# Down projection of a conformer/SSD block: 16 of its 22 k tiles as seven block products in two passes, in place of eight

## The chip, the cores and the metric

The kernel runs on one core of a Trainium2 chip. The metric is the device time of one execution in microseconds (us). It was run three times: 1059.66, 1051.93 and 1051.59 us, with a median of 1051.93. One further execution was profiled, and all rows below come from it.

The engines are named as the profile names them: PE is the matrix engine (PEld its weight loads), DVE the vector engine, ACT the scalar engine, POOL the GpSimd engine, SP the engine that issues the weight loads. PSUM has eight banks of 128 x 512 fp32; SBUF is the working memory.

## The reference, cut to what matters

The whole is one block of a hybrid network: a gated convolution branch, a state-space branch, a mixing projection, and a feed-forward part. Only the last lines bear on the change:

```
h = rms_norm(x, ffn_pre_g[i])                       # x: 512 tokens x 1024
gt, up = jnp.split(h @ w_gate_up[i], 2, axis=-1)    # FFN_HIDDEN = 2816
f = (jax.nn.silu(gt) * up) @ w_down[i]              # 512 x 2816 @ 2816 x 1024
x = x + rms_norm(f, ffn_post_g[i])
```

The down projection is the last product. Its contraction has 2816 = 22 x 128 rows, the 22 k tiles.

## The kernel before, in words

**Three matmuls for one.** Each fp32 operand is split into a high part (a rounding copy on ACT) and a low part (the rest, a subtraction on DVE). `mm3` (L171) multiplies high x high, high x low and low x high into the same PSUM bank; these are the matmuls of L173, L174 and L175. So each 128 x 512 piece of weights costs one ACT copy and one DVE subtraction per tile of 128 x 1024 (L139 and L145, or L905 and L910 where the gate/up projection does it), and each k tile of the activation costs one of each at 128 x 512 (L1200, L1201). For some weight tiles the low part is formed differently: ACT writes the negated high part, and a DMA from POOL's queue adds the weights on top while it copies (L142 and L143, or L907 and L908).

**Order.** `ORDER` is the list of all weight tiles in the order of their loads. `w_raw` (L129) issues a load on SP's queue into one of five `raw` buffers (`RAW_BUFS`); a load waits until the tile five places before it has been read for the last time. The split tiles lie in two sets of buffers, five pairs `whi`/`wlo` and three pairs `chi`/`clo`, which `pair_of_tiles` (L889) hands out in turn. The program is written in a sequential order, and the framework places every instruction in its engine's queue: it takes what its own timing says is ready, and the written order decides between what is ready together. Within a queue an engine works in order. `not_before` (L166) ties the order of two instructions by hand.

**Gate/up projection.** Its 22 units u (L1181 to L1194) are already done as seven block products in place of eight: `prep_s` (L924) and `prep_a` (L918) form sums of weight blocks on DVE and their halves, and `product` (L953) accumulates one block product. The activations' sums are in 14 tiles of the pool `h2`. The result of silu(gate) x up is `f32`, 22 k tiles of 128 x 512 tokens.

**Down projection.** After unit 21 the pool `h2` is closed (L1209), and in its place come `xres` (the residual, loaded by ACT's queue at L1212), `gpost1`, and four buffers each for the halves of `f32`. The first two k tiles' halves (`f01`, L1195) and the first two weight tiles (L1205) are formed before the last products of the gate/up projection. All eight PSUM banks hold the output: four token tiles t times two halves n of the 1024 columns. For k = 0 to 18 all eight banks take a step (`f_step`, L1220: 24 matmuls of 128 x 512); for the last three k the loop runs over t and n, so that each bank is finished in turn. Each finished token tile is squared on ACT (`mean_sq`, L838), its scale is made on DVE and POOL (`factor`, L844: L848 and L849), multiplied by the gain (L1249), added to the residual (L1237) and stored (L1240).

Of the kernel before, what the change touches and what calls it, by code (L numbers as in the profile page):

```python
# [18 lines left out]
P = 128  # L19
T = 512  # L20
# [57 lines left out]
ADD_LO = (2, 3) + tuple(range(7, FF // P, 2))  # L78
GU_AHEAD = 5
MOV_AT = 192  # L80

TAPS_GLU = 12
TAPS = (6, 14, 18, 20, 20, 20, 20, 20)
# [16 lines left out]
ORDER += [("wd", _i) for _i in range(NF)]  # L100


ZZ_LAST = [("zz", 4 * _p + 3) for _p in range(G // 2 - 1)]
# [8 lines left out]
def block_kernel(ctx: ExitStack, tc: tile.TileContext, x, xT, x0, prm, hp, gp, w, out):  # L112
# [11 lines left out]

    raws, split, more_raw = {}, {}, []
    seq = {key: n for n, key in enumerate(ORDER)}
    GU = range(seq["gu", 0], seq["wd", 0])

    def w_raw(n):  # L129
        if n < len(ORDER) and n not in raws:  # L130
# [1051 lines left out]
    for u in range(NF):  # L1182
# [9 lines left out]
            x3(u)  # L1192
        prep_s(max(u + 1, 3))
        prep_a(max(u + 2, 4) if u else 3)  # L1194
    f01 = [t.rearrange("p (k t) -> p k t", k=2) for t in pair_of_tiles()]  # L1195
    fs = {}

    def f_halves(k, room):
        fs[k] = room
        act.copy(fs[k][0], f32[:, k, :])  # L1200
        dve.tensor_tensor(out=fs[k][1], in0=f32[:, k, :], in1=fs[k][0].bitcast(F32), op=ALU.subtract)  # L1201

    for k in range(2):
        f_halves(k, [f[:, k] for f in f01])
    wd_ahead = [w_split(seq[("wd", k)]) for k in range(2)]  # L1205
    v2(NF - 1)
    x4(NF - 1)
    mark["chain"] = False
    h2.close()  # L1209
    pf = ctx.enter_context(tc.tile_pool(name="pf", bufs=2))  # L1210
    xres = pf.tile([P, NT, D], F32, bufs=1, name="xres")
    nc.scalar.dma_start(xres, x2d.rearrange("(t p) d -> p t d", p=P))  # L1212
    gpost1 = pf.tile([P, D], F32, bufs=1, name="gpost1")
    nc.scalar.dma_start(gpost1, gp[1].partition_broadcast(P))

    def f_split(k):
        if k < NF and k not in fs:
            f_halves(k, [pf.tile([P, T], F32R, tag=f"f{p}", bufs=4, name=f"f{p}{k}") for p in "hl"])

    def f_step(ps, t, k, wt, ns=(0, 1)):  # L1220
        tok = slice((t % 2 * 2 + t // 2) * P, (t % 2 * 2 + t // 2 + 1) * P)
        tm_step(ps, t, k, NF, fs[k][0][:, tok], fs[k][1][:, tok], wt, ns)

    ps = tm_tiles("wd")
    last = 3
    for k in range(NF - last):
        wt = w_get("wd", k)
        for j in range(3):
            f_split(k + j)
        for t in range(NT):  # L1230
            f_step(ps, t, k, wt)
    ws = {k: w_get("wd", k) for k in range(NF - last, NF)}
    f_split(NF - 1)

    def store(t, mg, rs):
# [6 lines left out]
    for t in range(NT):  # L1242
        mg = pf.tile([P, D], F32, tag="mg", name=f"mgc{t}")
        for n, c in enumerate(cols2):
            for k in range(NF - last, NF):
                f_step(ps, t, k, ws[k], (n,))
        rs = scale_of(ps[t], pf, f"c{t}")
        for n, c in enumerate(cols2):
            dve.tensor_tensor(out=mg[:, c], in0=ps[t][n], in1=gpost1[:, c], op=ALU.mult)  # L1249
        if t:  # L1250
            store(t - 1, *done)
        done = (mg, rs)
    store(NT - 1, *done)


def _feature_major(wt, cols):
# [4 lines left out]
def _layout(inp):  # L1261
    x = inp["x"][0]
    w_in, pw, so = inp["w_in"][0], inp["conv_pw_w"][0], inp["ssm_out_w"][0]
    wo, wgu, wd = inp["w_out"][0], inp["w_gate_up"][0], inp["w_down"][0]
    zs = [_feature_major(w_in, slice(OFF_Z + g * GW, OFF_Z + (g + 1) * GW)) for g in range(G)]
    zd = np.concatenate([zs[0].reshape(P, NK, GW), _feature_major(w_in, slice(OFF_DT, OFF_GATE)).reshape(P, NK, H)], axis=2)
    strips = {
        "val": (w_in, 0), "glu": (w_in, D), "x": (w_in, OFF_XBC), "B": (w_in, OFF_B),
        "C": (w_in, OFF_C), "gc": (w_in, OFF_GATE), "gs": (w_in, OFF_GATE + D), "pw": (pw, 0),
    }  # L1270
    rows = {"wo": wo, "wd": wd}

    def piece(n, i):
        if n == "gu":
            u, j = i // 2, i % 2
            o = (u % 2) * FF + (u // 2) * 2 * P
            one, two = [_feature_major(wgu, slice(o + q * P, o + (q + 1) * P)) for q in range(2)]
            return one if j == 0 else two
        if n in strips:
            a, o = strips[n]  # L1280
            return _feature_major(a, slice(o + i * P, o + (i + 1) * P))
        if n == "zd":
            a = zd[:, 3 * i : 3 * i + 3].reshape(P, -1)
            return np.pad(a, ((0, 0), (0, D - a.shape[1])))
        if n == "z":
            return zs[1][:, i * D : (i + 1) * D]
        if n == "zz":
            a = [zs[2 * (i // 4) + 2 + j].reshape(P, NK, GW)[:, 2 * (i % 4) : 2 * (i % 4) + 2] for j in range(2)]
            return np.concatenate(a, axis=2).reshape(P, -1)
        if n == "so":  # L1290
# [43 lines left out]
```

## Time and profile before

| what | value |
|---|---|
| times of three runs | 1059.66, 1051.93, 1051.59 us |
| span of the profiled execution, first to last instruction | 1050.4 us |
| granted PE clock over the span | 0.999 |
| PE busy | 1040.4 us (99%) |
| PEld busy | 908.2 us (86%) |
| DVE busy | 764.4 us (73%) |
| ACT busy | 602.8 us (57%) |
| POOL busy | 89.3 us (9%) |
| DMA moved | 141.35 MB, mean 135 GB/s |
| first and last matmul of the down projection start | 923.97 and 1043.44 us |

The profile gives no time for the profiled execution besides its span; the two shorter runs are 1.2 and 1.5 us above that span, which is what lies around the first and last instruction.

How to read it: an instruction's duration runs from its start to its results being written, and the next instruction of the same engine starts a little before that. So what an engine can do in a stretch is counted by the distance from start to start, and what a dependent instruction waits for by the whole duration. In a row of a timeline, the first number is the start in us, the second the length in us, and a bracket at the end gives the idle time of the engine before it and what ended it. In a table of windows, each engine's busy us and, in brackets, its instructions stand behind the length of the window.

### The profile page before, as it was taken

What the parts mean: (1) busy time and instruction counts of PE and PEld (TensorE: products, weight loads), DVE (VectorE), ACT (ScalarE), POOL (GpSimd) and SP (SyncE); (2) the same over time, 40 slices, a digit from 0 to 9 for tenths busy, and PEclk for the clock granted to TensorE, in tenths of its full rate; (3) what the DMA queues carried; (4) which work ended last, traced back from release to release, by engine and by line L of the source; (5) the groups of instructions that cost most, each with busy time, mean ns of one, the idle gap of its engine ahead of it and who ended that gap; (6) DMA issues with size and microseconds to landing.
All of it is one profiled execution on the core that took longest, in us unless ns stands there. A gap on an engine that the chain in (4) does not pass through costs nothing.

```text
span 1050.4 us, 15167 instructions
## 1 busy us (share of the span) xinstructions
PE 1040.4 (99%) x5893; PEld 908.2 (86%) x5893; DVE 764.4 (73%) x1114; ACT 602.8 (57%) x1011; POOL 89.3 (9%) x114
## 2 busy tenths in 40 slices
PE   9999999999999999999999999999999999999997
PEld 7898889888888888888888888889999999988886
DVE  7899976968595969596976555479997987643334
ACT  7655978684867476834432582376675665533322
POOL 0101101110111011101000000010000000000000
PEclk9999999999999999999999999999999999999999
DMA  8567644656445545554353223434565453352202
GB/s 295 152 168 213 149 102 120 180 138 163 122 139 149 134 141 139 140 141 120 87 134 101 80 79 103 161 114 127 170 189 144 126 163 114 101 209 94 98 1 80
DMA packets 39816, 141.35 MB, mean 135 GB/s; under 512 B 4544, under 2 KB 5568, under 8 KB 38720
## 3 DMA queue, kind: packets, MB, share of 16 engines
q1 hardware_dynamic: 28656, 97.32, 27.6%
q0 software_dynamic: 8352, 34.61, 16.8%
q10 hardware_dynamic: 2736, 8.46, 2.2%
q8 instruction: 46, 0.75, 0.3%
q14 instruction: 26, 0.21, 0.1%
HBM read 136.10 MB, written 4.26 MB: 134 GB/s over the span
## 4 chain that ended last, share of the span: by engine, by line
PE 94%; DVE 3%; ACT 1%; DMA 0%; issue 0%; SPq 0%; POOL 0%; DVEq 0%; POOLq 0%; ACTq 0%
PE tm_wd L175 4%; PE tm_wd L174 4%; PE tm_wd L173 4%; PE xy L173 3%; PE xy L174 3%; PE xy L175 3%; PE pso L173 3%; PE px L175 3%; PE px L173 3%; PE pso L175 3%; PE pso L174 3%; PE px L174 3%; PE yd L613 3%; PE pz L174 2%; PE pz L175 2%; PE pz L173 2%
## 5 line engine op out<-in xcount | busy, mean ns | idle before, releaser
L139 ACT CAST whi<-raw 128x1024 fp32r<-128x1024 f32 (+2 forms) x138 | 138.0, 1011 | 187.7 <-PE pC L174 39.8
L423 DVE SCALAR_TENSOR_TENSOR a<-v,prm_t,a 128x511 f32<-128x511 f32 (+15 forms) x240 | 180.7, 755 | 10.6 <-ACT a L420 7.9
L145 DVE TENSOR_TENSOR wlo<-raw,whi 128x1024 fp32r<-128x1024 f32 (+2 forms) x98 | 112.9, 1156 | 56.7 <-ACT whi L139 55.2
L143 POOL DMA_DIRECT2D wlo<-in_w x40 | 35.7, 892 | 363.5 <-ACT jk L649 91.8
L173 PE MATMUL tm_wd<-whi,fh 128*128 128x512 f32 x160 | 62.2, 389 | 0.0
L174 PE MATMUL tm_wd<-wlo,fh 128*128 128x512 f32 x160 | 62.2, 389 | 0.0
L175 PE MATMUL tm_wd<-whi,fl 128*128 128x512 f32 x160 | 62.2, 389 | 0.0
L174 PE MATMUL pz<-wlo,hhi 128*128 128x512 f32 (+2 forms) x160 | 56.1, 353 | 0.1
L175 PE MATMUL pz<-whi,hlo 128*128 128x512 f32 (+2 forms) x160 | 56.0, 352 | 0.0
L173 PE MATMUL pz<-whi,hhi 128*128 128x512 f32 (+2 forms) x160 | 55.6, 354 | 0.0
L1201 DVE TENSOR_TENSOR fl<-f,fh 128x512 fp32r<-128x512 f32 x20 | 13.8, 691 | 50.3 <-ACT fh L1200 50.3
L173 PE MATMUL px<-hhi,whi 128*128 128x512 f32 x128 | 50.2, 392 | 0.0
L175 PE MATMUL px<-hhi,wlo 128*128 128x512 f32 x128 | 49.9, 390 | 0.0
L174 PE MATMUL pso<-yl,whi 128*128 128x512 f32 x128 | 49.8, 389 | 0.0
L174 PE MATMUL px<-hlo,whi 128*128 128x512 f32 x128 | 49.8, 389 | 0.0
L175 PE MATMUL pso<-yh,wlo 128*128 128x512 f32 x128 | 49.7, 389 | 0.0
L173 PE MATMUL pso<-yh,whi 128*128 128x512 f32 x128 | 49.6, 391 | 0.0
L905 ACT CAST whi_g<-raw 128x1024 fp32r<-128x1024 f32 x40 | 41.3, 1054 | 14.4 <-DVE raw L936 7.3
L1200 ACT CAST fh<-f 128x512 fp32r<-128x512 f32 x20 | 12.4, 620 | 60.4 <-PE tm_wd L174 60.4
L910 DVE TENSOR_TENSOR wlo_g<-raw,whi_g 128x1024 fp32r<-128x1024 f32 x34 | 41.2, 1223 | 5.1 <-ACT whi_g L905 5.0
L142 ACT ACTIVATE wlo<-whi 128x1024 fp32r<-128x1024 f32 x40 | 42.2, 1055 | 0.3
L406 ACT ACTIVATE L<-L,nacs 128x128 f32<-128x128 f32 x128 | 40.1, 391 | 3.4 <-POOL L L400 3.2
(458 smaller groups left out, 3207.8 us busy)
## 6 DMA issues: line engine op xcount, KB each, us to landing
raw<-in_w SPq DMA_DIRECT2D x176, 512.0 KB, 3.8
wlo<-in_w POOLq DMA_DIRECT2D x40, 512.0 KB, 5.8
L<-scr POOLq DMA_DIRECT2D x8, 1024.0 KB, 6.2
wlo_g<-in_w POOLq DMA_DIRECT2D x6, 512.0 KB, 6.5
xr<-in_x ACTq DMA_DIRECT2D x4, 512.0 KB, 5.6
x2d<-xr ACTq DMA_DIRECT2D x4, 512.0 KB, 2.6
clo_g<-in_w POOLq DMA_DIRECT2D x4, 512.0 KB, 5.9
xres<-x2d ACTq DMA_DIRECT2D x1, 2048.0 KB, 10.0
```

The lines of the kernel that those rows point to most:

```text
L139: act.copy(hi[:, c], src[:, c])
L142: act.activation(lo[:, c], hi[:, c].bitcast(F32), AF.Copy, scale=-1.0)
L143: mark["lo"] = pool.dma_start(lo[:, c], w[n][:, c].bitcast(F32R), accum_op=ALU.add)
L145: mark["wlo"] = dve.tensor_tensor(out=lo[:, c], in0=src[:, c], in1=hi[:, c].bitcast(F32), op=ALU.subtract)
L173: mark["pe"] = pe.matmul(ps, lh, rh, start=start, stop=False, skip_group_check=more)
L174: pe.matmul(ps, lh, rl, start=False, stop=False, skip_group_check=more)
L175: mark["pe3"] = pe.matmul(ps, ll, rh, start=False, stop=stop, skip_group_check=more)
L406: act.activation(L[:, h, c, :], L[:, h, c, :], AF.Exp, bias=nacs[:, c, HG * g + h : HG * g + h + 1])
L423: return dve.scalar_tensor_tensor(out=va[j][:, d:], in0=vs[j][:, : T - d], scalar=col("dw_w", j * KC + KC - 1 - d), in1=va[j][:, d:], op0= ...
L613: pe.matmul(yd[c // 2][:, c % 2, h, :], s["L"][:, h, c, :], s["xdt"][:, c, h, :], start=True, stop=True)
L905: a_ = act.copy(hi, src)
L910: d_ = dve.tensor_tensor(out=lo, in0=src, in1=hi.bitcast(F32), op=ALU.subtract)
```

## The change

Sixteen of the 22 k tiles are taken as four groups j of four tiles. In each group the tiles of even number are one half of the contraction, those of odd number the other; the 512 tokens and the 1024 columns are halved too. Of the eight products of halves seven remain, each of a sum of activation blocks with a sum of weight blocks (`quad`: 12 matmuls of 128 x 512, two k tiles, two token tiles, one column half). Each product is accumulated over all four j in its own pair of PSUM banks.

- Pass 1 has three products: `plain_1`, `third_1`, `second_1`, in banks A, C and B. Pass 2 has four: `first_2` in two new banks D, `plain_2` on top of A, `fourth_2` on top of C, `sum_2` in B again. Between the passes A is copied to SBUF by ACT, and B and C are folded into two SBUF tiles by DVE (`between`), which also frees B.
- The weights of the 16 tiles come as 24 loads in place of 16 (`w1`, `w2`: three blocks per j and pass); the other six k tiles are loaded as before.
- The sums are formed on DVE, partly in place in `f32` and in the `raw` tiles; one sum per j is kept in SBUF between the passes (`keep`).
- Every product needs halves of its weights (128 x 1024) and of its activations (128 x 512): `w_form`, `f_form`. In 11 of the 28 products (`plain_1` of j = 0, 2, 3, all `plain_2` and `fourth_2`) the low half of the weights is made by ACT and an adding DMA from POOL's queue.
- The products are listed in `steps`, and the forms of a step are written four steps ahead of its matmuls (`S_AHEAD`); `not_before` keeps the matmuls in the written order.
- Then the six remaining k tiles are added in the old manner, with the token tiles in the order 1, 3, 0, 2 and the column halves in the order 1, 0. For six of the eight banks a DVE instruction adds or subtracts an SBUF tile, and the squares are then taken from SBUF.
- The pool for `xres` and `gpost1` is opened after pass 2.

```diff
+NS2 = 4
+KS2 = 4 * NS2
+ORDER += [("w1", 3 * _j + _q) for _j in range(NS2) for _q in range(3)]
+ORDER += [("w2", 3 * _j + _q) for _j in range(NS2) for _q in range(3)]
+ORDER += [("wd", _i) for _i in range(KS2, NF)]
...
+    one, two = [f32[:, e : KS2 : 2, :] for e in range(2)]
+    def f_form(j, name, src, room=None):
+        hi, lo = F_[j, name] = room or f_room(f"{name}{j}")
+        act.copy(hi, src)
+        dve.tensor_tensor(out=lo, in0=src, in1=hi.bitcast(F32), op=ALU.subtract)
+    def w_form(j, name, src, again=None):
+        hi, lo = pair_of_tiles()
+        Wd[j, name] = hi, lo
+        act.copy(hi, src)
+        if again is not None:
+            act.activation(lo, hi.bitcast(F32), AF.Copy, scale=-1.0)
+            pool.dma_start(lo, w[again].bitcast(F32R), accum_op=ALU.add)
+        else:
+            dve.tensor_tensor(out=lo, in0=src, in1=hi.bitcast(F32), op=ALU.subtract)
...
+    def plain_1(j, room=None):
+        n, ra = w_next("w1", j, 0)
+        w_form(j, "a11", ra, n if j != 1 else None)
+        f_form(j, "b11", f_of(j, one, c1), room)
+    def third_1(j, tmp=None, room=None):
+        ...
+        dve.tensor_tensor(out=t3, in0=f_of(j, one, c2), in1=f_of(j, two, c2), op=ALU.subtract)
+        dve.tensor_tensor(out=rb_, in0=ra, in1=rb_, op=ALU.add)
+        f_form(j, "t3", t3, room)
+        w_form(j, "s3", rb_)
+    def second_1(j, room=None, kept=None):
+        dve.tensor_tensor(out=b12, in0=b12, in1=b11, op=ALU.subtract)
+        dve.tensor_tensor(out=b11, in0=b12, in1=f_of(j, two, c2), op=ALU.subtract)
+        dve.tensor_tensor(out=keep[j], in0=rb_, in1=rc, op=ALU.add)
+        f_form(j, "t2", b11, room)
+        w_form(j, "s2", keep[j])
+    def first_2(j):
+        dve.tensor_tensor(out=rb_, in0=rb_, in1=rc, op=ALU.add)
+        f_form(j, "t1", f_of(j, one, c2))
+        w_form(j, "s1", rb_)
+    def plain_2(j):
+        w_form(j, "a12", rd, n)
+        f_form(j, "b21", f_of(j, two, c1))
+    def fourth_2(j):
+        dve.tensor_tensor(out=b11, in0=b11, in1=f_of(j, two, c1), op=ALU.add)
+        w_form(j, "a22", rc, n)
+        f_form(j, "t4", b11)
+    def sum_2(j):
+        dve.tensor_tensor(out=keep[j], in0=keep[j], in1=rd, op=ALU.add)
+        w_form(j, "s4", keep[j])
+        f_form(j, "b22", f_of(j, two, c2))
...
+    def quad(j, ps, wn, fn, start, stop, more=False):
+        for i in range(2):
+            c = slice(i * T, (i + 1) * T)
+            for e in range(2):
+                tok = slice(e * P, (e + 1) * P)
+                last = mark["pe3"]
+                m = mm3(ps[e], fh[:, i, tok], fl[:, i, tok], wh[:, c], wl[:, c], ...)
+                not_before(m, last)
+    steps = [(plain_1, 0, go_p), (third_1, 0, go_t)]
+    for j in range(1, NS2):
+        steps += [(plain_1, j, go_p), (second_1, j - 1, go_s), (third_1, j, go_t)]
+    steps += [(second_1, NS2 - 1, go_s)]
...
+    for t in (1, 3, 0, 2):
+        for n in (1, 0):
+            for k in range(NF - last_k, NF):
+                f_step(t, k, ws[k], n)
+            if (t, n) in extra:
+                dve.tensor_tensor(out=mg[:, cols2[n]], in0=of[n], in1=by, op=op)
+                of[n] = mg[:, cols2[n]]
+            ss.append(mean_sq(of[n], pt, f"c{t}", n))
+            dve.tensor_tensor(out=mg[:, cols2[n]], in0=of[n], in1=gpost1[:, cols2[n]], op=ALU.mult)
+        rs = factor(ss, f"c{t}")
```

More of the change, by code (lines that the diff above doesn't have):

```diff
@@ L80 @@
 MOV_AT = 192
+F_BUFS = 10
+S_AHEAD = 4
 TAPS_GLU = 12
@@ L1194, in block_kernel @@
         prep_a(max(u + 2, 4) if u else 3)
[L1195 to L1205, printed above, removed]
+    F_, Wd = {}, {}
+    one, two = [f32[:, e : KS2 : 2, :] for e in range(2)]
@@ L1209, in block_kernel @@
     h2.close()
     pf = ctx.enter_context(tc.tile_pool(name="pf", bufs=2))
-    xres = pf.tile([P, NT, D], F32, bufs=1, name="xres")
+    late = ExitStack()
+    pg = late.enter_context(tc.tile_pool(name="pg", bufs=1))
+    parts = [pf.tile([P, 2, T], F32, bufs=1, name=f"part{n}") for n in range(3)]
+    w2 = pg
+    def quad(j, ps, wn, fn, start, stop, more=False):
+        (wh, wl), (fh, fl) = Wd[j, wn], F_[j, fn]
+        for i in range(2):
[3 more added lines that the diff above has]
+                last = mark["pe3"]
+                m = mm3(ps[e], fh[:, i, tok], fl[:, i, tok], wh[:, c], wl[:, c], start and i == 0, stop and i == 1, more)
+                not_before(m, last)
@@ new lines, in block_kernel, with quad3 @@
+    B2 = []
+    def quad3(j):
+        if j == 0:
+            B2.extend(yd_tile(at_b[e], f"tm_b2{e}") for e in range(2))
+        quad(j, B2, "s4", "b22", j == 0, False)
+    for j in range(NS2):
+        steps += [
+            (first_2, j, quad5),
+            (plain_2, j, lambda j: quad(j, A, "a12", "b21", False, False, True)),
+            (fourth_2, j, lambda j: quad(j, C, "a22", "t4", False, False, True)),
+            (sum_2, j, quad3),
+        ]
+    for i, (_, j, go) in enumerate(steps):
+        ahead = i + S_AHEAD
+        for m in range(2 if i == 0 else ahead, ahead + 1):
+            if m < len(steps):
+                steps[m][0](steps[m][1])
+            elif m < len(steps) + 2:
+                w_split(seq["wd", KS2 + m - len(steps)])
+        go(j)
+        if go is go_p and j == NS2 - 1:
+            for e in range(2):
+                act.copy(parts[0][:, e], A[e])
+        if i == 3 * NS2 - 1:
+            between()
@@ L1227, in block_kernel @@
+    last_k = 3
+    for k in range(KS2, NF - last_k):
         wt = w_get("wd", k)
@@ L1229, in block_kernel @@
             f_split(k + j)
[L1230 to L1232 removed]
+        for t in (1, 3, 0, 2):
+            for n in range(2):
+                f_step(t, k, wt, n)
+    ws = {k: w_get("wd", k) for k in range(NF - last_k, NF)}
     f_split(NF - 1)
```

101 lines of the change are left out of this document (79 added, 22 removed).

## The prediction

> **What bounds the kernel now.** I read the page first (span, chain that ended last), then windows of 20 us over the down projection, then its first and last matmul, then the timelines of DVE, ACT and POOL around its start and end.
>
> ```profile
> span 1050.4 us, 15167 instructions
> PE 94%; DVE 3%; ACT 1%; DMA 0%; issue 0%; SPq 0%; POOL 0%; DVEq 0%; POOLq 0%; ACTq 0%
> ...
> 944.00:964.00 20.00, 20.00 (x90) 16.57 (x89) 6.80 (x8) 6.30 (x8) 0.00 (x0) 1.00 0.33 106
> 1004.00:1024.00 20.00, 20.00 (x90) 16.57 (x89) 6.45 (x7) 5.35 (x7) 0.00 (x0) 1.00 0.00 1
> ...
> L173 PE MATMUL tm_wd<-whi,fh 128*128 128x512 f32 x160 | 62.2, 389 | 0.0
> L173 PE MATMUL tm_wd<-whi,whi_g 128*128 128x512 f32 x16 | 6.2, 389 | 0.0
> ...
> 923.97 0.39 PE L173 MATMUL tm_wd<-whi,whi_g 128*128 128x512 f32 x1
> 1043.44 0.39 PE L175 MATMUL tm_wd<-whi,fl 128*128 128x512 f32 x1
> ```
>
> The chain is PE for 94% of the span. In the down projection PE is full in each window (20.00 of 20), while DVE is busy for a third of it (6.80, 6.45) and ACT no more. There are 3 x (160 + 16) = 528 matmuls (L174 and L175 have the same counts), and from the first start to the last lie 1043.44 - 923.97 = 119.47 us over 527 steps: 0.2267 us each. So nothing but the number of matmuls sets this stage.
>
> **What the change takes off PE.** Sixteen k tiles cost 16 x 24 = 384 matmuls; now 28 products of 12 are 336. That is 48 fewer: 48 x 0.2267 = **10.9 us**, if PE stays full. One product lasts 12 x 0.2267 = 2.72 us; pass 1 (12 products) 32.6 us, pass 2 (16) 43.5 us. The six other k tiles and their 144 matmuls stay.
>
> **What it adds to DVE and ACT.** Back to back, their costs are distances from start to start:
>
> ```profile
> 747.24 0.69 DVE L931 TENSOR_TENSOR s<-raw 128x512 f32<-128x512 f32 x1
> 747.84 0.69 DVE L936 TENSOR_TENSOR raw<-raw 128x512 f32<-128x512 f32 x1
> 749.98 1.22 DVE L910 TENSOR_TENSOR clo_g<-raw,chi_g 128x1024 fp32r<-128x1024 f32 x1
> 751.11 0.42 DVE L1082 TENSOR_TENSOR f<-xy,f 128x256 f32<-128x256 f32 x1
> ...
> 894.63 2.00 ACT L905 CAST chi_g<-raw 128x1024 fp32r<-128x1024 f32 x2
> 905.01 1.14 ACT L1200 CAST whi_g<-f 128x512 fp32r<-128x512 f32 x2
> ```
>
> DVE takes 0.60 us for 512 elements and 1.13 for 1024; ACT 2.00 - 1.05 = 0.95 for 1024 and 1.14 - 0.62 = 0.52 for 512. Per group j on DVE:
> - pass 1: `plain_1` one of 512 (0.60); `third_1` two of 512, two of 1024 (3.46); `second_1` three and two (4.06). Sum 8.12 against 3 x 2.72 = 8.16 on PE. For j = 1 comes one more of 1024.
> - pass 2: 2.86 + 0.60 + 1.20 + 2.86 = 7.5 against 10.9 on PE; the six instructions that fold banks (0.6 each) still fit.
>
> ACT: pass 1 2.42 + 1.47 + 1.47 = 5.4 per j, pass 2 1.47 + 2.42 + 2.42 + 1.47 = 7.8. So pass 2 has room on both engines, and **pass 1 has none on DVE**: 4 x 8.12 + 1.13 = 33.6 us for 32.6 us of PE. Of this, `plain_1` and `third_1` of j = 0 (4.1 us) are formed before the hand-over, where the old kernel formed two tiles each of f and weights (3.5 us); 29.5 us remain to be done before the twelfth product is due, 11 x 2.72 = 29.9 us in. DVE also had time before the hand-over:
>
> ```profile
> 914.72 0.42 DVE L1082 TENSOR_TENSOR f<-yv,f 128x256 f32<-128x256 f32 x1 [2.30 <-PE yv L175]
> 918.73 0.43 DVE L1082 TENSOR_TENSOR sg<-yv,sg 128x256 f32<-128x256 f32 x1 [3.58 <-PE yv L175]
> 921.52 0.42 DVE L1082 TENSOR_TENSOR f<-xy,f 128x256 f32<-128x256 f32 x1 [2.36 <-PE xy L175]
> ...
> 720.00:740.00 20.00, 18.78 (x156) 17.80 (x154) 19.74 (x33) 14.35 (x29) 0.00 (x0) 1.00 0.29 80
> 740.00:760.00 20.00, 19.76 (x174) 19.76 (x175) 20.00 (x33) 13.08 (x21) 0.00 (x0) 1.00 0.56 185
> 760.00:780.00 20.00, 20.00 (x179) 20.00 (x178) 20.00 (x31) 13.33 (x21) 0.89 (x1) 1.00 0.61 184
> ```
>
> The 8.2 us idle before 921.52 can take the sums that need neither a new buffer nor a product (the two in place in `f32` for j = 0, the weights' sum of `third_1` for j = 1: 2.3 us). And the start of the gate/up projection, the same kind of work, shows what PE loses beside a full DVE: DVE 59.74 of 60 us, PE 58.55. That is 1.45 us lost.
>
> **Where PE waits: the adding DMAs.** The low half that comes by POOL's queue has a long chain behind a load:
>
> ```profile
> raw<-in_w SPq DMA_DIRECT2D x18, 512.0 KB, 3.5
> ...
> 901.06 1.05 ACT L907 ACTIVATE clo_g<-chi_g 128x1024 fp32r<-128x1024 f32 x1
> 902.51 0.87 POOL L908 DMA_DIRECT2D clo_g<-in_w  x1 [22.57 <-ACT f L1145]
> ...
> DMA to landing us min/median/max: 5.4/5.9/6.7
> ```
>
> Load 3.5, high half 0.95, its negative 1.05, POOL's start 0.40 later (902.51 - 902.11), landing 5.9: 11.8 us from the moment at which a `raw` buffer comes free. With five buffers, tile 6 (`plain_1`, j = 2) takes the place of tile 1, which `second_1` of j = 0 reads last. That sum writes `keep`, which lies where `h2` was, and can end some 1.8 us after the hand-over if the sums before it were done early, up to 4 us if not. So the low half lands at 13.6 to 15.8 us, and the sixth product is due at 5 x 2.72 = 13.6 us: 0 to 2.2 us of waiting; I take 1.0. At the turn of the passes tile 14 (`plain_2`, j = 0) takes the place of tile 9, free after the sum of `third_1`, j = 3. From that sum to its own product lie a copy and a subtraction (1.05 + 1.22), then three products: 10.4 us against 11.8, so 1.4 us; I take 1.5. Later `plain_2` tiles have five products between (13.6 us and more) and wait for nothing. Bounds for all waiting: none, if DVE runs ahead; 5 us, if both chains meet their late ends and DVE adds the 1.45 us above. I take **2.5 us**, nearer the lower end, since DVE's margin (0.4 + 2.3 us) covers its own part.
>
> **The end.** The last token tile now finishes bank n = 0, whose square comes from PSUM as before.
>
> ```profile
> 1043.92 0.60 ACT L841 ACTIVATE jk_c<-tm_wd 128x512 bf16<-128x512 f32 x1 [1.35 <-PE tm_wd L175]
> 1044.64 0.21 DVE L848 TENSOR_SCALAR pm_c<-ss_c,ss_c 128x1 f32<-128x1 f32 x1 [1.13 <-ACT jk_c L841]
> 1044.77 0.68 DVE L1249 TENSOR_TENSOR mgc<-tm_wd,gpost 128x512 f32<-128x512 f32 x1
> 1045.00 0.54 POOL L849 TENSOR_TENSOR rs_c<-pm_c,neg_half 128x1 f32<-128x1 f32 x1 [3.54 <-DVE pm_c L848]
> 1045.58 1.42 DVE L1237 SCALAR_TENSOR_TENSOR xres<-mgc,rs_c,xres 128x512 f32<-128x512 f32 x2
> ```
>
> The multiplication by the gain waits for the square, as L848 does; it was written after L848 and ran behind it, beside POOL. Now it is written ahead of L848, so the chain may get its 0.6 us: between 0 and 0.6, I take 0.5. The added DVE instructions of the token tiles before (at most 3.9 us per 4.08 us of PE) stay behind PE. The eight more loads on SP's queue and the later load of `xres` on ACT's queue cost nothing: about 16 + 4 us of PE lie between the end of pass 2 and its first use. If ACT stood at that load until pass 2's last product, the halves of k tile 16 would be late by 0.62 + 0.69 = 1.3 us; their buffers are free long before, so they can stand ahead of it.
>
> **Sum.** 1050.4 - 10.9 + 2.5 + 0.5 = 1042.5 us of span. The median lies 1.5 us above the span of before, so **1044.0 us**.
>
> **Rivals.**
> *PE stays full.* DVE's early sums start the chain early enough, and the multiplication hides: 1050.4 - 10.9 + 0.3 + 1.5 = 1041.3. For it: the 760 to 780 row, where PE and DVE are both full. Against it: the 1.4 us at the turn.
>
> *The adding DMAs come late.* Pass 2 has eight of them and some 13 loads in 43.5 us.
>
> ```profile
> q1 hardware_dynamic: 28656, 97.32, 27.6%
> q0 software_dynamic: 8352, 34.61, 16.8%
> ...
> 764.82 0.89 POOL L908 DMA_DIRECT2D clo_g<-in_w  x1 [47.31 <-ACT sg L1172]
> DMA to landing us min/median/max: 5.5/5.5/5.5
> ...
> DMA to landing us min/median/max: 5.1/5.8/8.6
> ```
>
> By shares, one load of 0.524 MB takes 0.276 x 1050.4 x 0.524 / 97.32 = 1.56 us of all 16 DMA engines, one adding DMA 2.67 us (q0; other traffic is in it too): 13 x 1.56 + 8 x 2.67 = 42 of 43.5 us. The last two rows are the landing of the one issued at 764.82, and of those of the kernel's first half. If the landing stretches to 8.6 us, each place where the chain decides loses 2.7 us more; two of them, 5.4 us: 1049.4. Against it: in pass 1 and around it the queue is emptier, and pass 2 runs ahead from its fourth product on.
> On the Trainium skill's page "SBUF — State Buffer", section "SBUF: two separate sides", a DMA issued from GpSimd can stand still while VectorE holds a shared port, and its example goes from 620 to 3100 ns. By that, three deciding DMAs would lose 3 x 2.5 = 7.5 us (an estimate), and the time would be about 1051. The trace does not show it for subtractions: the DMA issued at 764.82, in a window with DVE at 20.00 of 20, landed in 5.5 us.
>
> *The written order wins (slower).* DVE and ACT work in order. Were their queues in written order, each sum, copy and subtraction would wait for the other engine: in pass 1 DVE would stand 1.3 us more at `plain_1` behind ACT's 2.42 us, and 0.65 us at each of two weight subtractions (1.05 + 0.03 against 0.60 between), so 10.8 us per j for 8.16 of PE; three such periods beyond the lead cost 7.8. At the turn the chain of 11.8 us starts behind `first_2`'s copies: 5. In pass 2 a period is 11.9 for 10.9: 4 x 1.05. Together 17 us in place of 2.5: 1058.5. It decides once PE waits over 10.4 us. Against it, the order that the queue of DVE had:
>
> ```profile
> L935 DVE TENSOR_TENSOR raw<-s,raw x2: 687/690/694, 893.0 to 900.7; 128x512 f32<-128x512 f32 x2
> L931 DVE TENSOR_TENSOR s<-raw x1: 692/692/692, 883.6 to 883.6; 128x512 f32<-128x512 f32 x1
> ```
>
> After 880 us two L935 are left but only one L931: the first sum of the last unit ran ahead of the unit before it. Queues are filled by readiness. For it: that readiness is a forecast, and pass 1 leaves no slack to a wrong one.
>
> **How the numbers follow.** Forecast (waits of 1 to 6 us, 1042 to 1048) 0.52; PE full 0.10; late DMAs 0.20; written order 0.18. The range of 1041.0 to 1054.0 holds the first three, and leaves out the last. A measurement of this kernel tells about 1% (10.5 us) from no change. Faster by more than that needs under 1041.4, so the PE-full case alone: 0.10. Slower by more than 1% needs 21 us of waiting, a part of the last case: 0.08. Within 1%: 0.82.
>
> **What would show it.** PE with 480 down-projection matmuls at 0.2267 us from start to start; windows of pass 1 with DVE above 19 of 20; PE's waits naming the adding DMA's tile at `plain_1` j = 2 and `plain_2` j = 0, together under 4 us; from the last matmul to the end 7 to 7.6 us (before 1050.4 - 1043.44 = 7.0). Wrong: PE waiting for DVE's or ACT's halves in every group of pass 1, or landing times above 8 us in pass 2.

## The result, and the profile after

The changed kernel takes 1056.86 us (median of 16 runs) beside 1052.01 for the kernel before (16 runs): a ratio of 1.0045, 95% interval [1.0026, 1.0064]. It is slower by half a per cent, clear of the noise. The forecast was 1044.0, with a range of 1041.0 to 1054.0. Five of these 16 executions and three of the 16 before are 5 to 8 us longer than the others (without them the medians are 1055.95 and 1051.93), and so are the profiled ones of two kernels below, without adding DMAs and with early additions, whose down projection starts 7 us later, so only differences within these two profiles are read. The profiled execution of the changed kernel has a span of 1055.0 us; every run lies 1.8 us above its span. Line numbers from here on are those of the changed kernel: the three matmuls are L179, L180 and L181.

First the engines' busy time and instructions on the page, and PE's waits in the list of waits (total us, times, longest one):

```profile
PE 1034.9 (98%) x5845; PEld 901.5 (85%) x5845; DVE 807.3 (77%) x1171; ACT 632.1 (60%) x1048; POOL 99.9 (9%) x125
```

```profile
PE tm_a L180 <- DMA wlo_g<-in_w: 8.1, 4, 3.7
PE tm_c L180 <- DMA wlo_g<-in_w: 0.3, 1, 0.3
```

PE has the 48 matmuls fewer (5893 before). It now waits 8.4 us, and each time for the low half of a weight that an adding DMA makes (the operand `wlo_g`). PE's timeline shows where, and what comes behind a wait:

```profile
924.26 0.39 PE L179 MATMUL tm_a<-whi_g,whi_g 128*128 128x512 f32 x1
...
937.88 0.39 PE L179 MATMUL tm_a<-whi_g,fh_b 128*128 128x512 f32 x1
940.14 0.50 PE L180 MATMUL tm_a<-wlo_g,fh_b 128*128 128x512 f32 x1 [1.88 <-DMA wlo_g<-in_w]
...
948.21 0.39 PE L179 MATMUL tm_a<-whi_g,fh_b 128*128 128x512 f32 x1
952.25 0.50 PE L180 MATMUL tm_a<-wlo_g,fh_b 128*128 128x512 f32 x1 [3.65 <-DMA wlo_g<-in_w]
...
953.85 0.63 PE L179 MATMUL tm_a<-whi_g,fh_b 128*128 128x512 f32 x1
954.28 0.63 PE L180 MATMUL tm_a<-wlo_g,fh_b 128*128 128x512 f32 x1
...
967.37 0.39 PE L179 MATMUL tm_a<-whi_g,fh_b 128*128 128x512 f32 x1
969.95 0.63 PE L180 MATMUL tm_a<-wlo_g,fh_b 128*128 128x512 f32 x1 [2.19 <-DMA wlo_g<-in_w]
...
1045.96 0.39 PE L181 MATMUL tm_a<-whi,fl_k 128*128 128x512 f32 x1
```

The three places are `plain_1` with j = 2 and j = 3, and `plain_2` with j = 0. From first to last start lie 1045.96 - 924.26 = 121.70 us; 479 steps of 0.2267 us would be 108.6, so **13.1 us are lost**. The three gaps, from start to start, exceed a step by 2.03, 3.81 and 2.35 us, two smaller ones (at 974 and 983) by 1.0 together: 9.2. Most of the rest is half clock: behind the second and the third gap seven and eight matmuls start 0.43 us apart, 0.20 too much, and one or two on each side of them are a little slow, about 3.5 us in all. The table of windows (us, PE, PEld, DVE, ACT and POOL busy with their instructions, clock, DMA share, GB/s) shows both:

```profile
930.00:940.00 10.00, 8.26 (x37) 6.52 (x35) 10.00 (x14) 6.24 (x8) 0.87 (x1) 1.00 0.81 239
...
950.00:960.00 10.00, 7.75 (x27) 6.25 (x28) 4.08 (x6) 3.94 (x6) 0.00 (x0) 0.83 0.55 181
...
970.00:980.00 10.00, 9.68 (x35) 7.55 (x36) 9.25 (x11) 7.00 (x9) 1.56 (x2) 0.83 1.06 290
```

PE is busy 9.68 of 10 us in the last row, yet with 35 matmuls in place of 44: there a full PE is one at a clock of 0.83. DVE is full in the first row, as forecast for pass 1, but stands still in the second.

The stage starts 0.3 us later, and the tail, from the last matmul's start to the end of the span, is 2.1 us longer (1055.0 - 1045.96 = 9.04 against 6.96). The sum is -10.9 + 13.1 + 0.3 + 2.1 = +4.6, which is the difference of the spans. (The expectations below count 13.4 us of waiting, with the 0.3.)

Why the low halves are late, by the landing of the adding DMAs and of the loads around them (minimum, median, maximum), and by ACT's, DVE's and POOL's timelines:

```profile
DMA to landing us min/median/max: 5.6/8.8/10.7
DMA to landing us min/median/max: 3.5/5.6/12.0
```

```profile
941.14 1.05 ACT L1218 CAST whi_g<-raw 128x1024 fp32r<-128x1024 f32 x1 [0.55 <-DMA raw<-in_w]
...
943.70 0.88 POOL L1221 DMA_DIRECT2D wlo_g<-in_w  x1 [8.29 <-ACT wlo_g L1220]
...
955.37 0.59 ACT L1355 COPY part<-tm_a 128x512 f32<-128x512 f32 x1 [6.50 <-PE tm_a L181]
957.79 0.69 DVE L1213 TENSOR_TENSOR fl_t<-f,fh_t 128x512 fp32r<-128x512 f32 x1 [5.92 <-ACT fh_t L1212]
958.17 1.05 ACT L1218 CAST whi_g<-raw 128x1024 fp32r<-128x1024 f32 x1
...
961.03 1.05 ACT L1220 ACTIVATE wlo_g<-whi_g 128x1024 fp32r<-128x1024 f32 x1
962.48 0.88 POOL L1221 DMA_DIRECT2D wlo_g<-in_w  x1 [17.91 <-ACT wlo_g L1220]
```

The forecast took 5.9 us of landing and 3.5 of loading; from 905 us on they were 8.8 and 5.6 in the median. At the three places the landings were 5.6, 8.5 and 7.5 us (from the issues at 934.54, 943.70 and 962.48 to PE's first use), so the first was no longer than forecast. At `plain_1` j = 3 the DMA issued at 943.70 landed at 952.2. While PE waited for it, ACT stood 6.50 us at the copy of A (L1355), which reads the result of this very product; all the halves of the next steps were queued behind it, and so `plain_2` j = 0 began its own chain only at 958.17. Between its copy and its negative (961.03) ACT made two other copies, 1.9 us that the forecast's chain does not have. In this kernel one late landing thus delayed the next chain.

### The profile page after: what moved, and what is told of

Same layout as the page of the kernel before. It is cut to its first block, busy times and chain, and to the rows that moved or that the text cites. A ratio compares the mean times of both kernels' runs of the same rounds, so it can differ in the third digit from the quotient of the medians.

```text
span 1055.0 us, 15197 instructions
## 1 busy us (share of the span) xinstructions
PE 1034.9 (98%) x5845; PEld 901.5 (85%) x5845; DVE 807.3 (77%) x1171; ACT 632.1 (60%) x1048; POOL 99.9 (9%) x125
## 4 chain that ended last, share of the span: by engine, by line
PE 82%; ACT 5%; DVE 5%; issue 4%; DMA 2%; POOL 1%; SPq 0%; ACTq 0%; POOLq 0%; DVEq 0%
PE xy L181 3%; PE xy L179 3%; PE xy L180 3%; PE pso L179 3%; PE pso L181 3%; PE pso L180 3%; PE yd L619 3%; PE pz L180 2%; PE pz L181 2%; PE pz L179 2%; PE yv L181 2%; PE yv L180 2%; PE yv L179 2%; PE px L181 2%; PE px L179 2%
## 5 line engine op out<-in xcount | busy, mean ns | idle before, releaser
L145 ACT CAST whi<-raw 128x1024 fp32r<-128x1024 f32 (+2 forms) x122 | 121.3, 1005 | 193.3 <-PE pC L180 39.8
L151 DVE TENSOR_TENSOR wlo<-raw,whi 128x1024 fp32r<-128x1024 f32 (+2 forms) x82 | 93.3, 1143 | 60.3 <-ACT whi L145 58.9
L180 PE MATMUL pz<-wlo,hhi 128*128 128x512 f32 (+2 forms) x160 | 56.4, 354 | 0.1
L181 PE MATMUL pz<-whi,hlo 128*128 128x512 f32 (+2 forms) x160 | 56.1, 352 | 0.0
L179 PE MATMUL pz<-whi,hhi 128*128 128x512 f32 (+2 forms) x160 | 55.7, 354 | 0.0
L179 PE MATMUL px<-hhi,whi 128*128 128x512 f32 x128 | 50.3, 393 | 0.0
L181 PE MATMUL px<-hhi,wlo 128*128 128x512 f32 x128 | 49.9, 390 | 0.0
L180 PE MATMUL pso<-yl,whi 128*128 128x512 f32 x128 | 49.9, 390 | 0.0
L180 PE MATMUL px<-hlo,whi 128*128 128x512 f32 x128 | 49.9, 389 | 0.0
L181 PE MATMUL pso<-yh,wlo 128*128 128x512 f32 x128 | 49.7, 390 | 0.0
L179 PE MATMUL pso<-yh,whi 128*128 128x512 f32 x128 | 49.6, 392 | 0.0
L513 DVE SCALAR_TENSOR_TENSOR x<-px,prm_t,x 128x511 f32<-128x511 f32 (+2 forms) x48 | 35.2, 743 | 1.0 <-ACT x L511 0.7
L180 PEld LDWEIGHTS pz<-wlo,hhi 128*128 128x128 f32 x160 | 30.2, 189 | 4.3 <-DVE wlo L151 0.7
L179 PEld LDWEIGHTS pz<-whi,hhi 128*128 128x128 f32 x160 | 30.2, 189 | 3.9
L181 PEld LDWEIGHTS pz<-whi,hlo 128*128 128x128 f32 x160 | 30.2, 189 | 3.7
L513 DVE SCALAR_TENSOR_TENSOR C<-pC,prm_t,C 128x511 f32<-128x511 f32 (+2 forms) x24 | 17.9, 744 | 19.1 <-ACT C L511 18.8
```

Source lines behind the costliest of these rows:

```text
L145: act.copy(hi[:, c], src[:, c])
L151: mark["wlo"] = dve.tensor_tensor(out=lo[:, c], in0=src[:, c], in1=hi[:, c].bitcast(F32), op=ALU.subtract)
L179: mark["pe"] = pe.matmul(ps, lh, rh, start=start, stop=False, skip_group_check=more)
L180: pe.matmul(ps, lh, rl, start=False, stop=False, skip_group_check=more)
L181: mark["pe3"] = pe.matmul(ps, ll, rh, start=False, stop=stop, skip_group_check=more)
L513: dve.scalar_tensor_tensor(out=a[:, d:], in0=ps[:, : T - d], scalar=col("ssm_w", i * KS + KS - 1 - d), in1=a[:, d:], op0=ALU.mult, op1=ALU ...
```

## The experiments

All times stand beside the kernel before, run on the same chip (1052.2 to 1052.3 us in the three groups). "Lost" is the time from the first to the last start of the stage's matmuls less 479 steps of 0.2267 us: 13.1 us in the changed kernel.

**What the adding DMAs cost in all.**

```diff
             act.activation(lo, hi.bitcast(F32), AF.Copy, scale=-1.0)
-            pool.dma_start(lo, w[again].bitcast(F32R), accum_op=ALU.add)
```

> The adding DMAs of the down projection are left out (11 of them): the low half of those weights is then only the negated high half. ACT's work stays. Theory 1: PE waits for under 2 us in all and never at half clock; the end is as in the changed kernel; 1043 to 1047. Theory 2: DVE still sets the end of pass 1, PE waits for DVE's halves there; 1050 or more.

1044.67 us, ratio 0.9912 [0.9885, 0.9939]: a time of the first theory. This kernel leaves out the adding DMAs and keeps ACT's part. PE's only wait in the stage, the first and the last matmul, and a window of pass 1:

```profile
PE tm_b L180 <- DVE clo_g L1222: 0.8, 1, 0.8
```

```profile
931.39 0.39 PE L179 MATMUL tm_a<-whi_g,whi_g 128*128 128x512 f32 x1
...
1041.12 0.39 PE L181 MATMUL tm_a<-whi,fl_k 128*128 128x512 f32 x1
```

```profile
944.00:954.00 10.00, 10.00 (x46) 8.29 (x45) 10.00 (x13) 6.31 (x9) 0.00 (x0) 1.00 0.62 215
```

DVE is as full as before (10.00) and PE loses nothing beside it in this window. The stage takes 109.73 us, so 1.1 are lost in place of 13.1. The adding DMAs thus cost some 12 us: 12.0 by the stage, 12.2 by the medians. Of the rest of the change only the tail, 9.08 us here, is not as forecast.

**One deciding place taken away: the low halves of `plain_1` j = 2, 3 on DVE.**

```diff
-        w_form(j, "a11", ra, n if j != 1 else None)
+        w_form(j, "a11", ra, n if j == 0 else None)
```

> Only the low halves of plain_1 for j = 2 and 3 change: a subtraction on DVE in place of ACT's negative and the adding DMA. Theory 1 (the waits come from the adding DMAs' chain behind a load): the 1.9 and 3.7 us of PE's wait at these two products go, with the matmuls at half clock behind the second; DVE gets 2.3 us more in pass 1, of which PE sees 1 to 3. Time 1049 to 1053. Theory 2 (DVE is full in pass 1 and sets its end whatever the DMAs do): PE waits for DVE's halves by as much as it waited for the DMAs; time 1055 to 1059.

1053.49 us, 1.0008 [0.9976, 1.0039]: just above the first theory's times. Both waits of pass 1 turn into three lags of DVE and ACT, 2.6 us together, which the first theory allowed; the wait at the turn stays, and is longer (2.8 us against 2.2):

```profile
PE tm_a L180 <- DMA wlo_g<-in_w: 3.2, 2, 2.8
PE tm_b L180 <- DVE clo_g L1223: 1.0, 1, 1.0
PE tm_b L179 <- ACT chi_g L1218: 0.9, 1, 0.9
PE tm_c L180 <- DVE clo_g L1223: 0.7, 1, 0.7
```

**The copy of A placed later in ACT's queue**, behind the halves that are written ahead of it (`mark["act"]` is the last copy of an activation's high half):

```diff
-        if go is go_p and j == NS2 - 1:
-            for e in range(2):
-                act.copy(parts[0][:, e], A[e])
         if i == 3 * NS2 - 1:
+            for e in range(2):
+                not_before(act.copy(parts[0][:, e], A[e]), mark["act"])
             between()
```

> Only ACT's copy of the two A banks moves: behind the halves of the first four products of pass 2 in ACT's queue. Theory 1 with its second part (that copy stands at the head of ACT's queue until the late product ends, 6.5 us, and holds back pass 2's halves): the wait at the first product j = 3 stays at 3.7 us, but DVE's 5.9 us of idle time at the turn and the 2.2 us wait at plain_2 of j = 0 go, with its half clock; 1052 to 1054.5. Rival (pass 2 waits because the DMA engines are full, whenever its DMAs start): no change, 1056 to 1058.

1058.89 us, 1.0054 [1.0023, 1.0085]: no gain.

```profile
PE tm_a L180 <- DMA wlo_g<-in_w: 4.6, 2, 3.7
PE tm_c L180 <- DMA wlo_g<-in_w: 2.2, 1, 2.2
```

`plain_2` j = 0 now waits for nothing, as the first theory said, but a new wait of 2.2 us stands at `fourth_2` j = 0. In pass 1 the longest wait, 3.7 us, is at `plain_1` j = 2 and none at j = 3, though nothing was changed ahead of these places: single waits differ by 1.8 us and more between two such profiles. The copy passes a delay on; without it another adding DMA is late all the same, and why it is late was not followed.

**Half the bytes of each adding DMA.**

```diff
-            pool.dma_start(lo, w[again].bitcast(F32R), accum_op=ALU.add)
+            pool.dma_start(lo[:, :512], w[again][:, :512].bitcast(F32R), accum_op=ALU.add)
```

> The eleven adding DMAs move and add only the first 512 of 1024 columns; the second half of those low halves stays the negated high half. The number of DMAs, their order and their releases stay. Theory 1 (the landing is long because the 16 DMA engines are shared by adding DMAs and loads): the DMA share in 965 to 995 falls from 1.0 to about 0.75, landings of the adding DMAs fall from 5.6 to 10.7 us to 3 to 6 us, the waits from 13.4 to 2 to 6 us: 1046 to 1050. Theory 2 (a landing is mostly a fixed latency of issue and queue, whatever the bytes): landings stay above 5.5 and up to 9 us, the time at 1053 to 1057.

1051.02 us, 0.9985 [0.9966, 1.0005]. The adding DMAs of 934 to 1000 us, first as changed, then with half of the bytes, with their median landing:

```profile
wlo_g<-in_w POOLq DMA_DIRECT2D x8, 512.0 KB, 8.9
```

```profile
wlo_g<-in_w POOLq DMA_DIRECT2D x8, 256.0 KB, 6.3
```

256 KB less take 2.6 us off the landing, so of 8.9 us some 5.2 go with the bytes (an estimate that takes the relation as straight) and 3.7 do not. In the quieter stretches that the forecast used, 512 KB landed in 5.4 to 6.7 us, so some 3 us of the 8.9 come with the density of this one. PE's waits fall from 8.4 to 4.5 us, of which 1.9 are for ACT and 2.6 for the adding DMAs, and 8.8 us are lost. Neither theory has it all: the time is just above what sharing alone should give, below what a fixed latency should.

**The deciding places of both passes moved to DVE, and the additions done early.**

```diff
-        w_form(j, "a11", ra, n if j != 1 else None)
+        w_form(j, "a11", ra, n if j == 0 else None)
...
-        w_form(j, "a12", rd, n)
+        w_form(j, "a12", rd, n if j else None)
...
-        w_form(j, "a22", rc, n)
+        w_form(j, "a22", rc, n if j else None)
```

(and the edit of the early additions, below)

> The low halves of plain_1 for j = 2 and 3, of plain_2 and fourth_2 for j = 0 are made by DVE instead of by ACT's negative and an adding DMA (seven adding DMAs are left of eleven), and the six extra additions of the tail are made in the PSUM banks after the first k tile of the plain part. Theory 1 (what the change loses is the late landing of the adding DMAs, worst where pass 2 begins): the waits for DMA in front of plain_1 j = 2, j = 3 and plain_2 j = 0 (8.9 us of gaps and about 4 us at half clock in the changed kernel) become lags of DVE of at most 1 us each, the tail is 1.3 us shorter as with the early additions alone: 1047 to 1050. Theory 2 (DVE is already full, each low half costs it 1.13 us, and PE waits for DVE in every group instead): 1052 to 1056. Theory 3 (the wait moves on to the next adding DMA, as with the late copy): one wait for DMA of 2 us and more at plain_2 or fourth_2 with j = 1, 1050 to 1053.

1055.15 us, 1.0033 [1.0009, 1.0058]: a time of the second theory, with the third one's wait, and with lags of DVE and ACT of 4.3 us in four places besides, the longest of which is shown:

```profile
PE tm_a L180 <- DMA wlo_g<-in_w: 4.0, 1, 4.0
PE tm_c L179 <- DVE part L1321: 1.8, 1, 1.8
```

With `plain_2` and `fourth_2` of j = 0 on DVE, `plain_2` of j = 1 waits 4.0 us and half clock follows. This DMA was issued only at 972.82: on ACT its copy stood behind that of `first_2`, which waited 4.22 us, until 969.32, for a sum of DVE (L1261). So the wait moved on to the next `plain_2`, and a late start of the chain had its part in it.

**All eleven low halves on DVE.**

```diff
-        w_form(j, "a11", ra, n if j != 1 else None)
+        w_form(j, "a11", ra, None)
...
-        w_form(j, "a12", rd, n)
+        w_form(j, "a12", rd)
...
-        w_form(j, "a22", rc, n)
+        w_form(j, "a22", rc)
```

> All eleven low halves of the stage are made by DVE, with no adding DMA and no negative on ACT; the rest as in the changed kernel. DVE gets 11 times 1.13 = 12.4 us more in about 108 us, where it is already busy 10.00 of 10 in most windows. Theory 1 (late DMAs are the loss, DVE has slack of some us in queue depth): PE waits for DVE by 4 to 9 us in all, 1048 to 1053, and the waits stand at many groups of pass 2 instead of at three. Theory 2 (DVE is the real bound of the stage, the DMAs only hid it): the full 12.4 us and more come back as waits, 1056 to 1060.

1048.97 us, 0.9962 [0.9944, 0.998]: 0.4% faster than the kernel before, at the lower end of the first theory's times. 5.6 us are lost. PE's waits are the last three rows of the first experiment on `plain_1`, at the same places (0.7, 0.9, 1.0 us), and there are none in pass 2, not the many that the first theory put there:

```profile
954.00:964.00 10.00, 8.10 (x28) 5.95 (x27) 10.00 (x13) 7.73 (x12) 0.00 (x0) 0.83 0.55 168
...
984.00:994.00 10.00, 10.00 (x45) 8.27 (x45) 10.00 (x12) 6.91 (x10) 0.00 (x0) 1.00 0.53 157
```

DVE is at 10.00 of 10 in every window from 934 to 1004 us, with 12.4 us more to do, and keeps up; it does not stand still between 950 and 960 any more.

**The same low halves by a subtraction on POOL.**

```diff
-            act.activation(lo, hi.bitcast(F32), AF.Copy, scale=-1.0)
-            pool.dma_start(lo, w[again].bitcast(F32R), accum_op=ALU.add)
+            pool.tensor_tensor(out=lo, in0=src, in1=hi.bitcast(F32), op=ALU.subtract)
```

> The eleven low halves that adding DMAs make are made by a subtraction on POOL (raw minus high half, 128x1024), with no negative on ACT and no adding DMA; the rest as in the changed kernel. POOL's select over 128x2048 takes 2.07 us in the changed kernel's profile, so the subtraction should take 1 to 3 us, against 5.6 to 10.7 us of landing. Theory 1 (the landing alone is late): nearly all the 13.4 us of waiting go, and ACT has 0.95 us less per weight: 1043 to 1046. Theory 2 (a two-input subtraction on POOL keeps DVE from its own operands for as long as it runs, DVE is full, and PE waits for DVE): DVE's 128x1024 operations beside it take 1.5 times as long and more, 1049 to 1056.

1057.91 us, 1.005 [1.0035, 1.0065], from four runs: above the times of both theories. POOL's subtraction, and two of DVE's groups beside it (total us, mean ns):

```profile
L1220 POOL TENSOR_TENSOR wlo_g<-raw,whi_g 128x1024 fp32r<-128x1024 f32 x8 | 26.4, 3308 | 55.3 <-ACT whi_g L1218 55.3
...
L1213 DVE TENSOR_TENSOR fl_t<-f,fh_t 128x512 fp32r<-128x512 f32 x11 | 11.9, 1079 | 0.0
L1222 DVE TENSOR_TENSOR clo_g<-raw,chi_g 128x1024 fp32r<-128x1024 f32 x4 | 9.2, 2309 | 0.0
```

```profile
PE tm_b L180 <- DVE clo_g L1222: 3.2, 1, 3.2
```

It is the second theory's way: DVE's subtractions in these groups take 1.08 and 2.31 us in the mean in place of 0.69 and 1.22, and PE's longest wait is for one of them.

**More time for a landing: the low half of the weights last in each product.**

```diff
-        for i in range(2):
...
-            for e in range(2):
...
-                m = mm3(ps[e], fh[:, i, tok], fl[:, i, tok], wh[:, c], wl[:, c], ...)
+        for n, (l, r) in enumerate([(fh, wh), (fl, wh), (fh, wl)]):
+            for i in range(2):
...
+                for e in range(2):
...
+                    m = pe.matmul(ps[e], l[:, i, tok], r[:, c], ...)
```

> The changed kernel with the twelve matmuls of each block product in another order: the four that need neither low half first, then the four with the low half of the activations, then the four with the low half of the weights. All else stays, the eleven adding DMAs too. A low half of the weights is then needed 8 matmuls, 1.8 us, after the first of its group instead of 0.23 us. Theory 1 (late landings are the loss, and waits of 2.2 us and more bring half clock after them): the gaps of 2.26, 4.04 and 2.58 us shrink by about 1.6 us each to about 0.7, 2.5 and 1.0 us, the half clock goes for most of them, 1048 to 1052. Theory 2 (the DMA engines are the bound of pass 2, a wait only moves on): the later groups wait instead, 1054 to 1057.

1052.32 us, 0.9999 [0.997, 1.0029].

```profile
951.39 1.27 PE L1304 MATMUL tm_a<-wlo_g,fh_b 128*128 128x512 f32 x4 [4.07 <-DMA wlo_g<-in_w]
970.98 1.20 PE L1304 MATMUL tm_c<-wlo_g,fh_t 128*128 128x512 f32 x4 [1.37 <-DMA wlo_g<-in_w]
```

The waits at `plain_1` j = 2 and `plain_2` j = 0 go, but 6.6 us of 8.4 stay: 4.1 at `plain_1` j = 3, where PE comes earlier but the DMA lands 28.1 us after the stage's first matmul as before (28.0), and 2.5 at two later groups. 9.3 us are lost in place of 13.1. The time is just above the first theory's, the manner half of the second's.

**The six extra additions early, in the banks.**

```diff
...
                 f_step(t, k, wt, n)
+                if k == KS2 and (t, n) in extra:
+                    by, op = extra.pop((t, n))
+                    dve.tensor_tensor(out=ps[t][n], in0=ps[t][n], in1=by, op=op)
```

> Only the six last additions move: DVE adds or subtracts the SBUF tiles in the PSUM banks themselves, after the first of the six remaining k tiles, when DVE has little to do; the end is then as in the old kernel (squares and gain straight from PSUM). If the 2 us by which the end is longer come from these additions queued on DVE behind stores that wait for POOL, the last matmul stays where it was and the end shrinks from 9.0 to 7.0 us: 1054 to 1055.5. If PE has to wait for the banks instead, no gain: 1056 to 1058.

1055.55 us, 1.0018 [0.9993, 1.0044]. From the last matmul's start (1053.14) to the end of the span (1060.9) lie 7.76 us against 9.04, and the stage loses 13.2 us, as before. First the tail of the changed kernel, then POOL's last step here:

```profile
1041.83 1.08 POOL L855 TENSOR_TENSOR rs_c<-pm_c,neg_half 128x1 f32<-128x1 f32 x1 [4.57 <-DVE pm_c L854]
1044.56 0.92 POOL L855 TENSOR_TENSOR rs_c<-pm_c,neg_half 128x1 f32<-128x1 f32 x1 [1.65 <-DVE pm_c L854]
1045.51 0.75 DVE L1400 SCALAR_TENSOR_TENSOR xres<-mgc,rs_c,xres 128x512 f32<-128x512 f32 x1 [0.44 <-POOL rs_c L855]
1046.18 0.68 DVE L1415 TENSOR_TENSOR mgc<-tm_c,part 128x512 f32<-128x512 f32 x1
...
1048.00 0.60 ACT L847 ACTIVATE jk_c<-tm_a 128x512 bf16<-128x512 f32 x1 [0.32 <-ACT jk_c L847]
1048.72 0.69 DVE L1418 TENSOR_TENSOR mgc<-tm_a,gpost 128x512 f32<-128x512 f32 x1 [0.31 <-ACT jk_c L847]
1049.68 0.54 POOL L855 TENSOR_TENSOR rs_c<-pm_c,neg_half 128x1 f32<-128x1 f32 x1 [4.20 <-DVE pm_c L854]
```

```profile
1055.52 0.54 POOL L855 TENSOR_TENSOR rs_c<-pm_c,neg_half 128x1 f32<-128x1 f32 x1 [3.60 <-DVE pm_c L854]
```

In the changed kernel the addition for bank n = 1 of the last token tile (L1415) stands in DVE's queue behind the first half of the store of the tile before (L1400), which waits for POOL; so the last square starts 2.04 us after the last matmul, against 0.48 in the kernel before. Without additions there it starts after 0.71. What stays of the tail's growth, 0.8 us, is mostly the 0.6 us of the multiplication (L1418) ahead of POOL's step.

**The best of these together**: all low halves on DVE and the early additions.

> All eleven low halves on DVE and the six extra additions done early in the banks, the order of the matmuls as in the changed kernel: beside c2 it gives what the order of the matmuls is worth. Theory 1: 1.3 us under all low halves on DVE alone, 1046.5 to 1048.5. Theory 2 (DVE, full until the end of the stage, makes the six early additions late): 1048.5 to 1051.

**1047.84 us, 0.9932 [0.9903, 0.996]**, 0.7% faster than the kernel before: a time of the first theory. The gain on the kernel with all low halves on DVE is the tail's (7.72 us against 9.09); 5.5 us are lost, as there. The three lags are as above, and PE's longest wait is now at `fourth_2` j = 0, whose bank C DVE has still to read. A window with two of the lags stands below its row of the waits:

```profile
PE tm_c L179 <- DVE part L1321: 1.8, 1, 1.8
```

```profile
954.00:964.00 10.00, 8.07 (x35) 6.14 (x34) 10.00 (x12) 7.96 (x11) 0.00 (x0) 1.00 0.50 167
```

**With the low halves last as well**

> All eleven low halves on DVE, the six extra additions done early in the banks, and the low halves of the weights last in each block product. Theory 1 (what is left with all low halves on DVE is lags of 0.7 to 1.0 us behind DVE around 951 to 958 and half clock right behind them): the waits for DVE go, that for ACT's high half of 0.9 us stays, no half clock, the tail 1.3 us shorter: 1043 to 1046. Theory 2 (DVE is the bound there, and a lag only moves to the next group): 1046 to 1049.

1048.94 us, 0.9962 [0.9938, 0.9985], **and with `keep` summed first in `second_1`**

> As c2, and second_1 adds the two raw weights into keep before it takes the two differences of the activations. Theory 1 (ACT waits for keep, and with it the last group of pass 1): the wait of 0.9 us for ACT's high half goes, 0.3 to 1.0 us under c2. Theory 2 (the differences, now later, are what ACT and DVE need next): same as c2 or up to 1 us slower.

1047.93 us, 0.9947 [0.9917, 0.9977]. The first is at the upper end of its second theory's times. The second is 1.0 us under the first, which its first theory named, but the intervals overlap, and the wait for ACT that was to go stays. In the waits both follow the second theory: what is saved at the three lags comes back as waits for DVE and ACT next to them (the first kernel's two waits are shown; the second has 2.9 us for the bank that DVE reads and 1.9 us for ACT):

```profile
PE tm_b L1304 <- ACT chi_g L1218: 1.9, 1, 1.9
PE tm_c L1304 <- DVE part L1323: 1.5, 1, 1.5
```

With 5.8 us lost in each, against 5.5 above, neither the order of the matmuls nor that of the sums brought the stage anything. That DVE's work then sets the end of pass 1 fits its 10.00 of 10 us there; no run with less of it was made.

## Why the prediction was wrong, by its steps

**The 10.9 us off PE** were right: 48 matmuls fewer, and without the adding DMAs the stage takes 109.73 us in place of 119.47, which is 10.9 less 1.1 of waiting. That this kernel's 1044.67 us lie so near the forecast of 1044.0 is partly luck: its waiting is smaller than forecast, its tail longer.

**DVE without margin in pass 1** was right: it is full there, and PE waits 0.8 us for it when the adding DMAs are gone.

**The waiting, 2.5 us with bounds of 0 and 5, is the step that failed.** It was 13.1, with the half clock behind the waits. The mechanism, a long chain behind a load that ends in an adding DMA, was the right one, and PE waited at both places that were named; its size was wrong. Four things made it so.
- The landing was taken at 5.9 and the load at 3.5 us, from the kernel's quieter parts; here 8.8 and 5.6 in the median, and at the three places 5.6, 8.5 and 7.5 for the landing. So 4.2 us of the 13.1 are longer landings at these places. The rival of the late adding DMAs held just this, with 42 of 43.5 us of DMA work in pass 2, and got 0.20; its sign, landings above 8 us in pass 2, came. The runs without the DMAs (some 12 us back) and with half of their bytes (2.6 us less landing) show it was the case.
- Only two places were examined. `plain_1` j = 2 waited 1.88 us, inside its own bounds of 0 to 2.2, and `plain_2` j = 0 2.19 against 1.5; `plain_1` j = 3, which no sentence named, waited 3.65 us, the longest of all. The same chain runs once for each j, and one j was worked out.
- ACT's queue was not costed at the turn. The copy of A stands at the head of ACT's queue until the product of `plain_1` j = 3 is done, so a late product delays the next chain. The experiment that moved it shows no gain in time, so its own price stays open. Two other copies ahead of the negative of `plain_2` j = 0 cost its chain 1.9 us more.
- Half clock behind a wait was not in the sum: about 3.5 us. With it and the third place the rival's own price, 1049.4, was too low as well.

**The tail, 0.5 us, was 2.1.** The 0.6 of the multiplication came as named; most of the rest came from the addition queued behind a store, which the prediction called hidden because it counted the work per token tile and not the order of DVE's queue. The early additions took 1.3 us of the tail away; 0.2 stay unexplained.

**The rival of the written order** named a time, 1058.5 us, that lies nearest to the 1056.86, and a total of waiting, 17 us, nearer to 13.1 than the forecast's. That is luck for the most part. It put the waits on DVE's and ACT's halves in every group, and the list of waits has none of these; with the same written order and no adding DMAs 1.1 us are lost. Its part on the turn, a chain that starts behind other copies of ACT, did happen.

On the port that DVE and POOL share, the Trainium skill's page "SBUF — State Buffer", section "SBUF: two separate sides", says that a VectorE instruction with two SBUF inputs and a GpSimd one that reads SBUF exclude each other for a whole instruction. The run with the subtraction on POOL agrees: there DVE's 1.22 us became 2.31 in the mean. Whether DVE also holds up the adding DMAs themselves was not tested by itself; the one issued at 934.54 landed in 5.6 us beside a full DVE, which speaks against it, and the landing fell with the bytes. The split between bandwidth, sharing with loads and the 3.7 us that do not go with the bytes was not taken further apart.

## What to carry to other kernels

A chain that is hidden at one density of work is to be costed with the landing times of the dense stretch, at every repetition, and with what its wait holds back in other queues. A wait costs its length, and often half clock behind it, some 1.7 us each time here. Where a transfer is there to relieve a busy engine, try that engine first: DVE, full in all of pass 2, took 12.4 us more work, and some 7 to 8 of the 12 us that the transfers had cost came back.

## What the runs showed of the hardware

- PE can go to half clock after short waits: behind 2.19 us of waiting (the row at 969.95) the matmuls start 0.43 us apart for 3.4 us or so; behind 1.88 us (940.14) they do not. The Trainium skill's page "TensorE: Matmul & The Clock Gate", section "HAM oscillation — how this bites in real kernels", gives idle gaps of over about 3.4 us as the rule; here less was enough. With all low halves on DVE the clock of 954 to 964 was 0.83 around lags of 0.9 and 1.0 us, and with the early additions, around the same lags, 1.00. With half of the bytes, half clock came behind a wait of 1.88 us (at 970.02); with `keep` summed first it did not come behind 1.9 and 2.9 us (at 956.11 and 967.53; the clock from 953 to 975 was 1.00). So no length of a wait decides alone, and what does was not found.
- POOL's step on 128 x 1 elements takes 0.54 us alone and 0.92 and 1.08 us at two places of the changed tail, where DVE works from two SBUF tiles beside it; with the early additions, where DVE reads PSUM and SBUF, it is 0.54 again.
- POOL's subtraction of 128 x 1024 takes 3.31 us in the mean beside a busy DVE (2.48 the shortest), DVE's 1.22 where POOL does nothing beside it.
